# An encoder layer on one core: the first stage's GpSimd tile work on VectorE, two of VectorE's kinds on ScalarE, and level differences one level ahead

## The chip, the core and the metric

The kernel runs on one core of a Trainium2 chip. The core has TensorE (matrix products into PSUM), VectorE and ScalarE (elementwise work), GpSimd (elementwise work, SBUF only) and SyncE (SP), whose queue issues the DMAs here. The metric is the device time of one execution in microseconds.

## The reference

One layer of a bidirectional encoder for 2048 tokens of width 1024. Cut to what matters here:

```
z = rms_norm(x) @ w_in                           # 1024 -> 3424 columns
z_rwkv = z_rwkv + mu * (centred_shift(z_rwkv) - z_rwkv)   # centred_shift: mean of both neighbours
u  = tanh(0.5 * (w0 + tanh(w_lo) @ w_up))        # RWKV decay, as the kernel writes it: exp(-c * (u + 1))
bc = cumsum(log_a) inside a chunk                # GLA, 64 key columns, both directions
scores[i, j] = sum_d q[i, d] * k[j, d] * exp(bc[i, d] - bc[j, d])     # masked to the chunk
o = scores @ v + (q * exp(bc)) @ S
```

`z_rwkv` feeds eight RWKV heads, handled in pairs; the rest of `z` feeds four GLA heads. After the mixers come an output projection, a gated FFN and a gated embedding, each with a norm and a residual.

## The kernel before

Function `phase_a` is the first stage. It goes through the tokens in four quarters `q` of 512. Per quarter it norms and transposes `x` (`make_xn`), then takes 27 projections of 128 columns (`zmat`), each from high and low parts of weights and inputs: three products (`mm3`, lines 73 to 75) per 128-row slice. In the first quarter `weights` loads each slice of `w_in` raw, ScalarE rounds it to the high part (line 217), GpSimd subtracts for the low part (line 218), and both parts are stored to DRAM; the later quarters load them (lines 209 and 210).

`mixed` (lines 294 to 299) makes the shifted mix of a projection: GpSimd adds the two neighbours, VectorE scales the middle, VectorE joins both. It is called 15 times a quarter (60 in all). `rwkv_pair` handles two heads; in each direction ScalarE takes a tanh (line 411), VectorE adds one (line 412, 32 in all) and scans (line 414). `gla_head` makes the scores of one head by levels: the chunk of 128 is halved seven times (`LV`), and at each level the difference of the running sum `b` to the middle of its block is exponentiated (tile `f`) and multiplied with the queries (`qq`) and keys (`kz`); four 128x128 products give a score tile `pl`, and VectorE copies what belongs to the level into `sc` under a mask (line 544). At six levels GpSimd makes two differences of half width (lines 532 and 533), ScalarE the exponential (534), GpSimd the query product (535) and VectorE two key products (536, 537); at the finest level, which comes first, GpSimd's lines are 523, 524 and 526. There are 16 calls of `gla_head`.

Heads (`h`) and pairs (`p`) are interleaved by a list written out by hand (`ORDER`). On top of that the program is laid out with `tile.TileContext(nc, schedule_with_timeline_sim=True)`: a planner puts each engine's instructions in an order from estimated costs, and each engine's queue then keeps that order. Tiles of a pool with one `tag` share its buffers: `f` and `qq` have two, score banks `ps3` three, raw weights `wr` three. The last GLA heads of the last quarter run while the second stage (`phase_b`) starts; its solver uses GpSimd in lines 694 and 695.

Of the kernel before, what the change touches and what calls it, by code (L numbers as in the profile page):

```python
# [7 lines left out]
F32 = mybir.dt.float32  # L8
# [3 lines left out]
AF = mybir.ActivationFunctionType  # L12
ALU = mybir.AluOpType
# [7 lines left out]
TQ = 512  # L21
# [71 lines left out]
def phase_a(ctx, ctr, ctb, tc, k):  # L93

    nc = tc.nc
    V, S, G = nc.vector, nc.scalar, nc.gpsimd
# [15 lines left out]
    ps3 = pool("psd", 3, space=PSUM)  # L112
# [4 lines left out]
    mu1 = c.tile([128, 15], F32, name="mu1")  # L117
# [61 lines left out]
    LV = [64, 32, 16, 8, 4, 2, 1]  # L179

    prev = None
    for li, n in enumerate([128] + LV):
        nb = 128 // n
# [14 lines left out]
    kz = [c.tile([128, TQ], F32, name=f"kz{li}") for li in range(7)]  # L198
# [5 lines left out]
    def weights(ft, first):  # L204

        wh = wp.tile([128, KT, 128], F32R, tag="wh", name="wh")
        wl = wp.tile([128, KT, 128], F32R, tag="wl", name="wl")
        if not first:
            nc.sync.dma_start(wh.bitcast(F32), k.ws[0, ft])
            nc.sync.dma_start(wl.bitcast(F32), k.ws[1, ft])  # L210
            return wh, wl
        n = KT // 2
        for j in range(0, KT, n):
            wr = wp.tile([128, n, 128], F32, tag="wr", bufs=3, name="wr")
            js = slice(j, j + n)
            nc.sync.dma_start(wr, a["w_in"][ft, :, js])
            S.copy(wh[:, js], wr)
            G.tensor_sub(wl[:, js], wr, wh[:, js].bitcast(F32))
        nc.sync.dma_start(k.ws[0, ft], wh.bitcast(F32))
        nc.sync.dma_start(k.ws[1, ft], wl.bitcast(F32))  # L220
        return wh, wl
# [61 lines left out]
    def zmat(ft, x, zp=zp):  # L283

        wh, wl = weights(ft, k.q == 0)
        z = zp.tile([128, XW], F32, tag="z", name="z")
        for (c0, n), (xh, xl) in zip(NB, x):
            pz = ps.tile([128, 512], F32, tag="psz", name="pz")
            for j in range(KT):
                mm3(nc, pz[:, :n], wh[:, j], wl[:, j], xh[:, j], xl[:, j], j == 0, j == KT - 1)  # L290
            S.copy(z[:, c0:c0 + n], pz[:, :n])  # L291
        return z

    def mixed(z, i, out):
        s = pp.tile([128, TQ], F32, tag="s", bufs=2, name="s")
        G.tensor_add(s, z[:, 0:TQ], z[:, 2:TQ + 2])
        V.tensor_scalar(out, z[:, 1:TQ + 1], mu1[:, i:i + 1], None, op0=ALU.mult)
        V.scalar_tensor_tensor(out, s, muh[:, i:i + 1], out, op0=ALU.mult, op1=ALU.add)
        return out

# [45 lines left out]
    def rwkv_pair(q, p, x, lo):  # L346
# [3 lines left out]
        t = lambda tag, bufs=1: pp.tile([128, TQ], F32, tag=tag, bufs=bufs, name=tag)  # L350
# [50 lines left out]
        bv = t("out", 2)  # L401
# [3 lines left out]
        for d in range(2):  # L405
            pu = ps2.tile([128, 512], F32, tag="ps2", name="pu")
            dr = slice(64 * d, 64 * d + 64)
            nc.tensor.matmul(pu, wup[d][:, cs], tw[d], start=True, stop=False)
            nc.tensor.matmul(pu, wupl[dr, cs], tw[d][dr], start=False, stop=True)
            u = t("u", 2)  # L410
            S.activation(u, pu, AF.Tanh, bias=w0h[:, 4 * d + p:4 * d + p + 1], scale=0.5)
            V.tensor_scalar(u, u, 1.0, None, op0=ALU.add)
            rv = (lambda ap: ap) if d == 0 else (lambda ap: ap[:, ::-1])
            V.tensor_tensor_scan(rv(u), m64, rv(u), 0.0, op0=ALU.mult, op1=ALU.add)

            E = pp.tile([128, 8, 65], F32, tag="E", bufs=1, name="E")
            S.activation(E[:, :, 1 - d:65 - d], ch(u), AF.Exp, scale=-0.5 * KAPPA)
            G.memset(E[:, :, 64 * d:64 * d + 1], 1.0)
            S.activation(u, u, AF.Exp, scale=0.5 * KAPPA)
            e1 = 64 if d == 0 else 0  # L420
            S.copy(k.dT[:, p, d, 8 * q:8 * q + 8].unsqueeze(2), E[:, :, e1:e1 + 1])
            st = pp.tile([128, 8, 2, 64], F32, tag="st", bufs=2, name="st")
            V.tensor_mul(st[:, :, 0, :], ch(kk), E[:, :, d:64 + d])
            V.tensor_mul(st[:, :, 1, :], ch(r), E[:, :, 1 - d:65 - d])
            nc.sync.dma_start(k.d["ar"][p, d, :, 8 * q:8 * q + 8], st)
            st = pp.tile([128, 8, 2, 64], F32, tag="st", bufs=2, name="st")
            V.tensor_mul(st[:, :, 0, :], ch(P0), ch(u))
            V.tensor_mul(st[:, :, 1, :], ch(P1), ch(u))
            nc.sync.dma_start(k.d["bk"][p, d, :, 8 * q:8 * q + 8], st)
# [59 lines left out]
    def gla_head(q, h, b, q2, k2, vt):  # L489
        t = lambda tag, bufs=1: gp.tile([128, TQ], F32, tag=tag, bufs=bufs, name=tag)  # L490
        F_, B_ = slice(0, 64), slice(64, 128)
# [16 lines left out]
        tokmajor(kh, kt, ps3, "ps3")  # L508

        sc = t("sc")  # L510
        for li in (6, 0, 1, 2, 3, 4, 5):
            pl = ps3.tile([128, 512], F32, tag="ps3", name="pl")
            n = LV[li]
            tv = lambda ap: ap.rearrange("p (b t) -> p b t", t=2 * n)
            nb = TQ // (2 * n)
            bv, k2v, kv = tv(b), tv(k2), tv(kz[li])
            lhs = kz[li]
            rhs = t("qq", 2)
            f = t("f", 2)
            if li == 6:  # L520

                fv = tv(f)
                G.tensor_sub(fv[F_], bv[F_], bv[F_, :, 0:1].to_broadcast([64, nb, 2]))
                G.tensor_sub(fv[B_], bv[B_, :, 1:2].to_broadcast([64, nb, 2]), bv[B_])
                S.activation(f, f, AF.Exp, scale=0.0625)
                G.tensor_mul(rhs, f, q2)
                V.tensor_copy(kv[F_, :, 0:1], k2v[F_, :, 0:1])
                V.tensor_copy(kv[B_, :, 1:2], k2v[B_, :, 1:2])
            else:
                mid = bv[:, :, n:n + 1].to_broadcast([128, nb, n])  # L530
                fv = tv(f)
                G.tensor_sub(fv[:, :, 0:n], mid, bv[:, :, 0:n])
                G.tensor_sub(fv[:, :, n:2 * n], bv[:, :, n:2 * n], mid)
                S.activation(f, f, AF.Exp, scale=0.0625)  # L534
                G.tensor_mul(rhs, f, q2)  # L535
                V.tensor_mul(kv[F_, :, 0:n], fv[F_, :, 0:n], k2v[F_, :, 0:n])
                V.tensor_mul(kv[B_, :, n:2 * n], fv[B_, :, n:2 * n], k2v[B_, :, n:2 * n])  # L537
            for j in range(4):
                js = slice(128 * j, 128 * j + 128)
                nc.tensor.matmul(pl[:, js], lhs[:, js], rhs[:, js], start=True, stop=True)  # L540
            if li == 6:
                V.tensor_tensor(w4(sc), w4(pl), mk7, op=ALU.mult)
            else:
                V.copy_predicated(w4(sc), msk[:, li, :].unsqueeze(1).to_broadcast([128, 4, 128]), w4(pl))
# [3 lines left out]
        for j in range(4):  # L548
            js = slice(128 * j, 128 * j + 128)
# [4 lines left out]
        for j in range(4):  # L554
            js = slice(128 * j, 128 * j + 128)
# [1012 lines left out]
```

## Time and profile before

| | |
|---|---|
| time, median of 3 runs (lowest, highest) | 3658.14 us (3655.13, 3660.93) |
| profiled execution: its own time, span | 3649.02 us, 3647.3 us |
| TensorE busy, weight loads busy | 3347.8 us (92%), 2856.6 us (78%) |
| VectorE busy | 2624.4 us (72%) |
| ScalarE busy | 1640.8 us (45%) |
| GpSimd busy | 978.7 us (27%) |
| chain that ended last, by engine | TensorE 66%, VectorE 17%, DMA 6%, ScalarE 5%, GpSimd 2% |

Busy time is the time in which an engine has an instruction of its own under way; the time in which its queue waits or issues is not counted. The chain is followed back from the last instruction, at each step to what released it or to the instruction before it on its engine. In the rows PE is TensorE, PEld its weight loads, DVE VectorE, ACT ScalarE, POOL GpSimd, SPq SyncE's queue; `L536` is line 536; `kz<-f,k` says which tile is written from which.

### The profile page before, as it was taken

To read this page: it belongs to the slowest core of one execution; us is meant where nothing else is said; L and a number is where in the kernel's file an instruction comes from. 1 tells how busy PE (TensorE), PEld (TensorE's weight loads), DVE (VectorE), ACT (ScalarE), POOL (GpSimd) and SP (SyncE) were. 2 spreads that over 40 slices of the span, in tenths; PEclk is the share of its full clock that TensorE was granted. 3 is DMA by queue.
4 is the path that set the end of the run, shared out by engine and by line. 5 is a ranking of instruction groups with operands and counts; after the bars stand their busy time and mean duration, and the time that the engine had idled before them with its cause. 6 is when DMAs were issued, how large, how long until landed. Compare 5 with 4: busy or idle time off the path is not lost.

```text
span 3647.3 us, 57330 instructions
## 1 busy us (share of the span) xinstructions
PE 3347.8 (92%) x20880; PEld 2856.6 (78%) x20880; DVE 2624.4 (72%) x4123; ACT 1640.8 (45%) x3451; POOL 978.7 (27%) x1348
## 2 busy tenths in 40 slices
PE   6888988988889899999969989999999999999998
PEld 6777877877878688898858868888788878787776
DVE  6888788788778467776763467777765566769887
ACT  5454445444444555656644453333433333324554
POOL 6854534534335144547401100000000000001112
PEclk9988999999998989999979999999999999999999
DMA  6655465465555445545255655555422234557775
GB/s 219 215 189 184 147 199 187 143 197 170 186 177 175 153 133 156 160 130 155 73 159 169 230 200 185 187 193 191 156 93 81 70 115 150 212 173 272 265 272 185
DMA packets 390439, 629.28 MB, mean 173 GB/s; under 512 B 122790, under 2 KB 223142, under 8 KB 390156
## 3 DMA queue, kind: packets, MB, share of 16 engines
q1 hardware_dynamic: 390156, 625.61, 52.3%
q8 instruction: 165, 2.70, 0.3%
q14 instruction: 118, 0.97, 0.1%
HBM read 403.18 MB, written 211.81 MB: 169 GB/s over the span
## 4 chain that ended last, share of the span: by engine, by line
PE 66%; DVE 17%; DMA 6%; ACT 5%; issue 4%; POOL 2%; SPq 1%; DVEq 0%; ACTq 0%; POOLq 0%
PE pB L73 6%; PE pB L75 6%; PE pB L74 6%; PE pA L74 5%; PE pA L75 4%; PE pA L73 4%; PE pC L74 4%; PE pC L75 4%; PE pC L73 4%; PE pg L662 3%; PE ph L781 3%; PE pf L798 2%; PE pz L75 2%; PE pz L73 2%; PE pz L74 2%
## 5 line engine op out<-in xcount | busy, mean ns | idle before, releaser
L1045 ACT CAST sh<-raws 128x512 fp32r<-128x512 f32 (+1 forms) x456 | 277.6, 610 | 667.0 <-PE pB L74 356.2
L73 PE MATMUL pz<-xh,wh 128*128 128x256 f32 (+1 forms) x1728 | 511.8, 297 | 26.7 <-ACT z L291 18.4
L75 PE MATMUL pz<-xh,wl 128*128 128x256 f32 (+1 forms) x1728 | 504.6, 295 | 6.0 <-DMA wl<-d_ws 4.1
L74 PE MATMUL pz<-xl,wh 128*128 128x256 f32 (+1 forms) x1728 | 504.5, 293 | 0.0
L1210 POOL TENSOR_TENSOR st<-st 128x1 f32<-128x1 f32 x64 | 18.0, 281 | 1631.2 <-ACT jk L1209 1630.7
L1046 DVE TENSOR_TENSOR sl<-raws,sh 128x512 fp32r<-128x512 f32 (+1 forms) x456 | 305.6, 671 | 112.9 <-ACT sh L1045 109.4
L73 PEld LDWEIGHTS pz<-xh,wh 128*128 128x128 f32 x1728 | 339.6, 197 | 40.3 <-ACT z L291 29.1
L75 PEld LDWEIGHTS pz<-xh,wl 128*128 128x128 f32 x1728 | 337.9, 197 | 15.1 <-DMA wl<-d_ws 6.8
L74 PEld LDWEIGHTS pz<-xl,wh 128*128 128x128 f32 x1728 | 340.1, 197 | 6.9 <-issue 5.8
L781 PE MATMUL ph<-x,wpi 128*128 128x128 f32 x1024 | 170.7, 295 | 8.9 <-ACT wpi L777 7.4
L73 PE MATMUL pA<-B11h,sh 128*128 128x512 f32 x360 | 147.7, 411 | 23.0 <-ACT B11h L1045 19.1
L540 PE MATMUL pl<-qq,kz 128*128 128x128 f32 x896 | 133.8, 296 | 32.4 <-DVE kz L537 30.9
L798 PE MATMUL pf<-sv,Ht 128*128 128x64 f32 x1024 | 152.3, 277 | 10.7 <-ACT sv L803 6.9
L540 PEld LDWEIGHTS pl<-qq,kz 128*128 128x128 f32 x896 | 121.2, 208 | 44.0 <-issue 30.2
L781 PEld LDWEIGHTS ph<-x,wpi 128*128 128x128 f32 x1024 | 139.8, 200 | 18.2 <-ACT wpi L777 12.9
L798 PEld LDWEIGHTS pf<-sv,Ht 128*128 128x128 f32 x1024 | 136.0, 196 | 22.5 <-ACT sv L803 10.4
L535 POOL TENSOR_TENSOR qq<-f,q 128x512 f32<-128x512 f32 x96 | 140.7, 1472 | 43.5 <-ACT f L534 24.2
L74 PE MATMUL pA<-B11l,sh 128*128 128x512 f32 x360 | 148.1, 411 | 3.3 <-DVE B11l L1046 3.3
L662 PE MATMUL pg<-ar,bk 64*128 64x128 f32 x1024 | 143.4, 297 | 6.0 <-DVE x L665 4.6
L75 PE MATMUL pA<-B11h,sl 128*128 128x512 f32 x360 | 146.7, 407 | 0.9 <-DVE sl L1046 0.9
L73 PE MATMUL pB<-T3h,sh 128*128 128x512 f32 x360 | 143.4, 398 | 0.0
L75 PE MATMUL pB<-T3h,sl 128*128 128x512 f32 x360 | 143.0, 397 | 0.0
(636 smaller groups left out, 9348.5 us busy)
## 6 DMA issues: line engine op xcount, KB each, us to landing
wh<-d_ws SPq DMA_DIRECT2D x81, 512.0 KB, 4.1
wl<-d_ws SPq DMA_DIRECT2D x81, 512.0 KB, 4.8
d_mt<-rawt SPq DMA_DIRECT2D x92, 256.0 KB, 2.5
raws<-in_ffn_gate SPq DMA_DIRECT2D x44, 512.0 KB, 4.4
raws<-in_ffn_up SPq DMA_DIRECT2D x44, 512.0 KB, 4.0
rawm<-d_mt SPq DMA_DIRECT2D x44, 512.0 KB, 8.6
d_hid<-c SPq DMA_DIRECT2D x88, 256.0 KB, 2.5
d_ar<-st SPq DMA_DIRECT2D x32, 512.0 KB, 2.9
```

The costliest lines, as they stand in the source:

```text
L73: nc.tensor.matmul(out, ah, bh, start=start, stop=False, **kw)
L74: nc.tensor.matmul(out, ah, bl, start=False, stop=False, **kw)
L75: nc.tensor.matmul(out, al, bh, start=False, stop=stop, **kw)
L535: G.tensor_mul(rhs, f, q2)
L540: nc.tensor.matmul(pl[:, js], lhs[:, js], rhs[:, js], start=True, stop=True)
L662: nc.tensor.matmul(pg[h][:, j], bk[HR[h], j], ar[HR[h], j], start=True, stop=True)
L781: nc.tensor.matmul(ph[:, h, j], w[:, h, j], x[:, j0 + j, 4 * h:4 * h + 2, :], start=True, stop=True)
L798: nc.tensor.matmul(pf[:, h, j0 + j], H[:, h, j], SV[p, d, c][:, h, j0 + j], start=True, stop=True)
L1045: nc.scalar.copy(hi, src)
L1046: nc.vector.tensor_sub(lo, src, hi.bitcast(F32))
L1210: G.tensor_add(st[:, 2:3], st[:, 0:1], st[:, 1:2])
```

## The change

All of it is in `phase_a`. Five edits:

- The low part of the weights is subtracted by VectorE in place of GpSimd.
- In `mixed`, VectorE adds the neighbours in place of GpSimd, and ScalarE scales the middle in place of VectorE.
- The add of one in `rwkv_pair` is done by ScalarE in place of VectorE.
- In the level loop of `gla_head` the differences and the query product are done by VectorE in place of GpSimd.
- The differences and the exponential of a level are made by a new function `diff`, which is called one level ahead: before the products of a level, the next level's `f` is begun. The score bank `pl` is asked for after the products.

```diff
--- before.py
+++ after.py
@@ -215,7 +215,7 @@
             js = slice(j, j + n)
             nc.sync.dma_start(wr, a["w_in"][ft, :, js])
             S.copy(wh[:, js], wr)
-            G.tensor_sub(wl[:, js], wr, wh[:, js].bitcast(F32))
+            V.tensor_sub(wl[:, js], wr, wh[:, js].bitcast(F32))
         nc.sync.dma_start(k.ws[0, ft], wh.bitcast(F32))
         nc.sync.dma_start(k.ws[1, ft], wl.bitcast(F32))
         return wh, wl
@@ -293,8 +293,8 @@
 
     def mixed(z, i, out):
         s = pp.tile([128, TQ], F32, tag="s", bufs=2, name="s")
-        G.tensor_add(s, z[:, 0:TQ], z[:, 2:TQ + 2])
-        V.tensor_scalar(out, z[:, 1:TQ + 1], mu1[:, i:i + 1], None, op0=ALU.mult)
+        S.activation(out, z[:, 1:TQ + 1], AF.Copy, scale=mu1[:, i:i + 1])
+        V.tensor_add(s, z[:, 0:TQ], z[:, 2:TQ + 2])
         V.scalar_tensor_tensor(out, s, muh[:, i:i + 1], out, op0=ALU.mult, op1=ALU.add)
         return out
 
@@ -409,7 +409,7 @@
             nc.tensor.matmul(pu, wupl[dr, cs], tw[d][dr], start=False, stop=True)
             u = t("u", 2)
             S.activation(u, pu, AF.Tanh, bias=w0h[:, 4 * d + p:4 * d + p + 1], scale=0.5)
-            V.tensor_scalar(u, u, 1.0, None, op0=ALU.add)
+            S.activation(u, u, AF.Identity, bias=k.one)
             rv = (lambda ap: ap) if d == 0 else (lambda ap: ap[:, ::-1])
             V.tensor_tensor_scan(rv(u), m64, rv(u), 0.0, op0=ALU.mult, op1=ALU.add)
 
@@ -508,33 +508,44 @@
         tokmajor(kh, kt, ps3, "ps3")
 
         sc = t("sc")
-        for li in (6, 0, 1, 2, 3, 4, 5):
-            pl = ps3.tile([128, 512], F32, tag="ps3", name="pl")
+        tv = lambda ap, n: ap.rearrange("p (b t) -> p b t", t=2 * n)
+
+        def diff(li):
+
             n = LV[li]
-            tv = lambda ap: ap.rearrange("p (b t) -> p b t", t=2 * n)
             nb = TQ // (2 * n)
-            bv, k2v, kv = tv(b), tv(k2), tv(kz[li])
+            f = t("f", 2)
+            fv, bv = tv(f, n), tv(b, n)
+            if li == 6:
+
+                V.tensor_sub(fv[F_], bv[F_], bv[F_, :, 0:1].to_broadcast([64, nb, 2]))
+                V.tensor_sub(fv[B_], bv[B_, :, 1:2].to_broadcast([64, nb, 2]), bv[B_])
+            else:
+                mid = bv[:, :, n:n + 1].to_broadcast([128, nb, n])
+                V.tensor_sub(fv[:, :, 0:n], mid, bv[:, :, 0:n])
+                V.tensor_sub(fv[:, :, n:2 * n], bv[:, :, n:2 * n], mid)
+            S.activation(f, f, AF.Exp, scale=0.0625)
+            return f
+
+        levels = (6, 0, 1, 2, 3, 4, 5)
+        nxt = diff(levels[0])
+        for i, li in enumerate(levels):
+            n = LV[li]
+            k2v, kv = tv(k2, n), tv(kz[li], n)
             lhs = kz[li]
             rhs = t("qq", 2)
-            f = t("f", 2)
+            f = nxt
+            if i < 6:
+                nxt = diff(levels[i + 1])
+            fv = tv(f, n)
+            V.tensor_mul(rhs, f, q2)
             if li == 6:
-
-                fv = tv(f)
-                G.tensor_sub(fv[F_], bv[F_], bv[F_, :, 0:1].to_broadcast([64, nb, 2]))
-                G.tensor_sub(fv[B_], bv[B_, :, 1:2].to_broadcast([64, nb, 2]), bv[B_])
-                S.activation(f, f, AF.Exp, scale=0.0625)
-                G.tensor_mul(rhs, f, q2)
                 V.tensor_copy(kv[F_, :, 0:1], k2v[F_, :, 0:1])
                 V.tensor_copy(kv[B_, :, 1:2], k2v[B_, :, 1:2])
             else:
-                mid = bv[:, :, n:n + 1].to_broadcast([128, nb, n])
-                fv = tv(f)
-                G.tensor_sub(fv[:, :, 0:n], mid, bv[:, :, 0:n])
-                G.tensor_sub(fv[:, :, n:2 * n], bv[:, :, n:2 * n], mid)
-                S.activation(f, f, AF.Exp, scale=0.0625)
-                G.tensor_mul(rhs, f, q2)
                 V.tensor_mul(kv[F_, :, 0:n], fv[F_, :, 0:n], k2v[F_, :, 0:n])
                 V.tensor_mul(kv[B_, :, n:2 * n], fv[B_, :, n:2 * n], k2v[B_, :, n:2 * n])
+            pl = ps3.tile([128, 512], F32, tag="ps3", name="pl")
             for j in range(4):
                 js = slice(128 * j, 128 * j + 128)
                 nc.tensor.matmul(pl[:, js], lhs[:, js], rhs[:, js], start=True, stop=True)
```

## Rows read from the trace of the kernel before

**Rows 1.** Windows: stretch, busy us of PE, PEld, DVE, ACT, POOL; clock, DMA, GB/s
```profile
0.00:345.00 345.00, 273.18 (x1864) 247.47 (x1865) 275.17 (x359) 170.42 (x333) 221.49 (x221) 0.92 0.60 199
345.00:617.00 272.00, 242.72 (x1735) 221.35 (x1734) 217.22 (x299) 127.32 (x244) 118.22 (x115) 0.94 0.55 176
...
sum 1190.00, PE 1026.88 PEld 928.01 DVE 946.40 ACT 561.97 POOL 574.96; mean PE 256.72 PEld 232.00 DVE 236.60 ACT 140.49 POOL 143.74
```

**Rows 2.** Chain of waits in the stage: by line, then first and last piece
```profile
by line: issue 7.7%; PE pz L75 6.3%; PE pz L73 6.2%; PE pz L74 6.1%; DVE kz L537 3.5%; PE pl L540 3.1%; DVE kz L536 3.1%; DVE sc L544 2.7%; DMA wl<-d_ws 2.3%; DMA d_bk<-st 2.3%; DVE bx L461 1.9%; DVE bx L460 1.6%; DVE u L414 1.6%; PE po L55
3437 pieces in order of time: start us, us, what
0.73 0.07 issue
...
1189.57 0.48 PE po L557 x2
```

**Rows 3.** Groups of GpSimd in the stage: busy us, mean ns, idle before
```profile
L535 POOL TENSOR_TENSOR qq<-f,q 128x512 f32<-128x512 f32 x96 | 140.7, 1472 | 43.5 <-ACT f L534 24.2 <-PE pl L540 19.1 <-ACT u L411 0.2
L532 POOL TENSOR_TENSOR f<-bx 128x256 f32<-128x256 f32 x96 | 88.7, 924 | 123.2 <-PE pt L305 62.2 <-DVE kz L537 59.1
L218 POOL TENSOR_TENSOR wl<-wr,wh 128x512 fp32r<-128x512 f32 x54 | 81.7, 1527 | 53.5 <-ACT wh L217 51.2 <-issue 2.1
L533 POOL TENSOR_TENSOR f<-bx 128x256 f32<-128x256 f32 x96 | 78.8, 821 | 0.0
L296 POOL TENSOR_TENSOR s<-z 128x512 f32<-128x512 f32 x60 | 72.6, 1209 | 143.8 <-ACT z L291 112.0 <-PE pb L400 27.1 <-DVE kr L298 4.0
L523 POOL TENSOR_TENSOR f<-bx 64x512 f32<-64x512 f32 x16 | 26.2, 1639 | 92.8 <-DVE bx L460 86.8 <-DVE kz L537 5.9
L526 POOL TENSOR_TENSOR qq<-f,q 128x512 f32<-128x512 f32 x16 | 25.7, 1607 | 19.5 <-ACT f L525 10.8 <-DMA q<-qk 7.1 <-PE pz L75 1.5
L524 POOL TENSOR_TENSOR f<-bx 64x512 f32<-64x512 f32 x16 | 25.2, 1572 | 1.1
```

**Rows 4.** VectorE: groups (mean), then lines (min/median/max ns, first and last start)
```profile
L536 DVE TENSOR_TENSOR kz<-f,k 64x256 f32<-64x256 f32 x96 | 68.0, 708 | 17.7 <-ACT f L534 17.3
L497 DVE TENSOR_TENSOR qh<-qh,q 128x512 f32<-128x512 f32 x16 | 15.8, 990 | 5.6 <-ACT qh L496 5.4
L440 DVE SCALAR_TENSOR_TENSOR qk<-cs,cv 128x512 f32<-128x512 f32 x32 | 22.3, 696 | 14.4 <-ACT cs L439 13.9
L271 DVE TENSOR_TENSOR xl<-pt,xh 128x512 fp32r<-128x512 f32 x24 | 16.0, 682 | 0.7 <-ACT xh L270 0.6
...
L536 DVE TENSOR_TENSOR kz<-f,k x96: 391/546/1506, 93.7 to 1177.4; 64x256 f32<-64x256 f32 x96
L440 DVE SCALAR_TENSOR_TENSOR qk<-cs,cv x32: 675/692/907, 67.1 to 1133.9; 128x512 f32<-128x512 f32 x32
L412 DVE TENSOR_SCALAR u<-u x32: 405/426/1519, 151.6 to 1088.9; 128x512 f32<-128x512 f32 x32
L297 DVE TENSOR_SCALAR r<-z,mu x16: 476/502/1505, 97.0 to 1056.5; 128x512 f32<-128x512 f32 x16
L497 DVE TENSOR_TENSOR qh<-qh,q x16: 679/935/1679, 82.4 to 1158.3; 128x512 f32<-128x512 f32 x16
```

**Rows 5.** Line 435 on ScalarE, min/median/max ns
```profile
L435 ACT ACTIVATE cv<-z,pv x32: 706/722/728, 63.5 to 1123.7; 128x512 f32<-128x512 f32 x32
```

**Rows 6.** Waits in the stage: us in total, times, longest (SP's: 0 to 345)
```profile
ACT f L534 <- POOL f L533: 132.8, 58, 6.1
PE pl L540 <- DVE kz L537: 30.9, 19, 4.5
PE pt L305 <- DVE v L298: 18.6, 6, 5.8
DVE kz L536 <- ACT f L534: 17.3, 15, 1.8
SPq L216 <- POOL wl L218: 25.0, 18, 5.2
```

## The prediction

> **What bounds the kernel now.** The page's busy line comes first: TensorE is busy 92% of the span, VectorE 72%, GpSimd 27%. That is an average, so the stage that the change touches is cut out. The last head of the first stage ends shortly after 1190 us, and 1190 us is the stage in all that follows. By windows [rows 1] its TensorE is busy 1027 us (weight loads 928), VectorE 946, ScalarE 562, GpSimd 575. The first window (0 to 345, where the weights are split) is the poorest: TensorE 273 of 345, GpSimd 221. The second is like the two that follow it: TensorE 243 of 272, VectorE 217. No engine is full; two are nearly so, and they wait for each other.
>
> Then the chain of waits in the stage [rows 2]. Its 3437 pieces, added up by engine, are VectorE 477 us, TensorE 376, DMA 95, ScalarE 94, "issue" 91, GpSimd 50. The reader is to see that the three TensorE lines of the projection have 6% each and that directly behind them stand VectorE's two key products of the level loop (L537, L536) and the copy under the mask (L544). VectorE has 1000 us of instructions in the stage when each of its 1311 is counted whole (946 where overlaps count once), so 477/1000 = 0.48 of its work lies on the path; ScalarE's share is 94/562 = 0.17.
>
> Third, GpSimd's groups [rows 3]. The eight kinds that leave are 81.7 + 72.6 + 26.2 + 25.2 + 25.7 + 88.7 + 78.8 + 140.7 = 540 of its 575 us; 35 us stay (roots, memsets, masks, the start of the solver). Last, what single VectorE instructions take [rows 4]. One and the same product L536 takes 391 ns at its shortest and 1506 at its longest, mean 708; the add L412 405 to 1519; L440, which mostly runs when GpSimd rests, 675, median 692. Laid beside GpSimd's spans, the long ones are those that overlap a GpSimd instruction. Two kinds of count give the stretch in all: mean less shortest, over 36 groups with more than half a microsecond (first L536, 68.0 - 96 x 0.391 = 30.5; last L440, 22.3 - 32 x 0.675 = 0.7), is 217 us; with the median of the instructions that meet no GpSimd work in place of the shortest it is 198.
>
> **The change part by part**, against the profiled execution (3649.0 us, span 3647.3; the median of the runs shown is 3658.1, 9.1 more).
>
> *VectorE, what leaves.* The stretch: 198 to 217 us; GpSimd keeps 35 of 575 us, so some 12 may stay, which makes the lower end 188. I take 200. The scaling in `mixed` (60 x 0.476 = 28.6) and the add of one (32 x 0.405 = 13.0) leave with their unstretched length, 42 us; their stretch is in the 200 already [rows 4].
>
> *VectorE, what arrives*, at unstretched lengths, since the partner of the stretching goes. Weight splitting 54 x 0.682, by the like subtraction L271, is 36.8. The neighbour sum in `mixed` 60 x 0.68 (L497 at its shortest, as are the next two) is 40.8; the query products 112 x 0.68 = 76.2; the two subtractions of the finest level 32 x 0.68 = 21.8. The subtractions of the other six levels have 256 columns: 192 x 0.41, just above L536's shortest, = 78.7. Together 254. Below, all at the shortest, it is 250; above, if the new ones were stretched as L536 (0.708) and L497 (15.8/16, 0.99) are now, 391.
>
> Net on VectorE: 254 - 42 - 200 = +12 us, of which 0.48 on the path: **+6**. The ends are 250 - 42 - 217 = -9 (-4 on the path) and 391 - 42 - 188 = +161 (+77); I stay near the low one, since with GpSimd silent the unstretched rows are the nearest.
>
> *GpSimd.* Of its 50 us on the path the moved lines have 45 (f L532 and L533 19, weights 12, products 7, `mixed` 4, finest level 3). It goes: **-45**. What took 0.92 + 0.82 + 1.47 us of GpSimd for a level [rows 3] is 0.41 + 0.41 + 0.68 of VectorE, already counted above. Between zero, if VectorE is just as late there, and -50.
>
> *ScalarE* gets 92 instructions. The nearest row is L435, a scaled copy of the same size with a column operand, 0.722 [rows 5]: 66 us, times 0.17 = **+11**; from 0 (VectorE's own sum runs beside the scaled copy) to all 66. Behind them in its queue stand the projection's evacuations, for which TensorE's next projection waits, so zero is too kind.
>
> What the row shows here is that the column form costs ScalarE 722 ns while VectorE did the two kinds in 476 and 405. The Trainium skill, "ScalarE: Activation LUTs", Rules for kernel authors, says that adds and multiplies belong on VectorE and not on ScalarE. By that rule these two edits lose 66 - 42 = 24 us of engine time, at one common share of 0.48 some 12 us on the path, and the whole sum would be -12. By the rows the engine with the smaller share on the path takes them (-20 + 11), and I go by the rows.
>
> *One level ahead.* ScalarE's exponential of the level loop (0.63 us) had to end before the query product could start; GpSimd's lateness alone cost ScalarE 132.8 us of waiting there, VectorE 17.3 behind the exponential and TensorE 30.9 behind the key products [rows 6]. Now the next level's differences stand ahead of this level's products, so the exponential runs beside 0.68 + 2 x 0.41 + 0.73 us of VectorE work. The 5 us of L534 on the path go: **-5**, from 0 to -17.
>
> *Waits that are added.* The weight subtraction stands on VectorE behind ScalarE's cast. What queues behind it is every head's and pair's work, and SP's loads and stores of weights wait for it as they did for GpSimd (25.0 us before the loads) [rows 6]. GpSimd waited 51.2 us for that cast [rows 3], VectorE in its own like case only 0.7 for 24 [rows 4]; I take under 2 us and keep 51 x 0.48 = 25 as the other end. With two buffers for the level's factor, a next difference must wait for the products of the level before; they are earlier in VectorE's own order, so this costs nothing. The score bank is asked for later, which holds it for less time.
>
> *Order.* The order on every engine is planned anew from estimated costs when the program is made. No row tells the new one; this widens the range alone.
>
> Sum: +6 - 45 + 11 - 5 = **-33 us**: 3616 in the profiled execution, 3625 on the scale of the median. What is late next is VectorE itself, busy about as long as before in a shorter stage, and then TensorE, 163 us idle in it.
>
> **The rivals.**
>
> *VectorE stays the bound.* Its idle 244 us of the stage [rows 1] are ended by TensorE and ScalarE, few of them by GpSimd itself. If that idle share stays and only the work counts, the stage grows with it: 1190 x 12/946 = +15, 3664, on the median's scale 3673. It decides as soon as the stretch is under 254 - 42 = 212 us, and my two counts lie on either side. For it: 946 is close to TensorE's weight loads, and the work of GpSimd was free parallel time. Against it: 45 us of GpSimd on the path and the 17 behind the exponential. The Trainium skill, "Perfetto Trace Analysis", Identifying the Most-Contended Engine, has the same as a rule: the engine with the highest occupancy binds, and TensorE is judged by its weight loads. By that rule the trace names VectorE (946 against 928), and the kernel gets slower. Chance 0.23.
>
> *TensorE is let go.* It waits 122 us for VectorE in the stage, 30.9 of them for the key products and 18.6 for `mixed` values before a transpose [rows 6]. If the first go wholly and the other 91 by half, that is -76: 3573, or 3582. For it: these waits are longest where the stretched instructions are. Against it: VectorE has no less to do. Chance 0.15.
>
> *Nothing to be measured.* The freed path is taken up at once by TensorE, busy 86% [rows 1], and the 45 us of GpSimd by VectorE in its place: 0 to -7, about 3655 on the median's scale. For it: VectorE's sum is level. Chance 0.12.
>
> **How the numbers follow.** Forecast 0.50 (its own range 3590 to 3650), rivals 0.23, 0.15, 0.12. A difference under 0.2% (7.3 us) can't be told from none. Faster: 0.50 + 0.15 = 0.65; the same 0.12; slower 0.23. The range takes in the rival with TensorE let go and 22 us below it, and on the other side the rival with VectorE as the bound: 3560 to 3680. Left out are the far ends of the costs, such as new instructions stretched as the old.
>
> **What would show it.** Right: GpSimd falls from 575 to about 35 us in the stage; L536 and the other all-SBUF groups have means near their shortest; VectorE's busy time stays within 30 us of 946; the wait of the key products on the exponential is gone; the stage ends near 1157. Wrong: stretched VectorE instructions without GpSimd; a VectorE sum of 1000 or more; new TensorE waits for the low weight parts or for ScalarE's evacuations; a stage that ends where it did, with TensorE's idle time unchanged. The rest of the span, 2457 us, should be the same.

## The result, and the profile after

The changed kernel takes 3533.5 us (median of 4 runs, 3530.5 to 3551.8), the one before 3659.5 (a fourth run added to the three above): a ratio of 0.967, 95% interval 0.964 to 0.969, so 126 us faster. Forecast were 3625 and a range from 3560. The direction was right, the size was not: nearly four times the 33 us of the sum.

All of it lies in the stage. In the two profiled executions 2450 us before and 2453 after lie between the last update of the state `SF` (line 558, now 569) and the end; that update is 120 us earlier. Two windows serve for reading what follows: up to 2 us before that update (1195 and 1075 us), and up to the fourth quarter's first cast of `tw` on ScalarE (line 322 in both; 889 and 784 us), before the second stage mixes in. In the runs further down the second window ends at the same cast; "up to the fourth quarter" means it. Columns are as in [rows 1]: stretch, busy us of TensorE, weight loads, VectorE, ScalarE, GpSimd; granted clock, DMA share, GB/s. First the kernel before, then the changed one, whose first two windows answer to the two of [rows 1].

```profile
0.00:889.00 889.00, 756.83 (x5335) 687.41 (x5335) 709.61 (x957) 423.59 (x819) 457.94 (x449) 0.94 0.56 183
0.00:1195.00 1195.00, 1031.88 (x7228) 931.78 (x7228) 949.60 (x1319) 562.71 (x1081) 579.10 (x587) 0.94 0.56 183
```

```profile
0.00:784.00 784.00, 722.12 (x5324) 660.52 (x5325) 689.79 (x1240) 473.78 (x892) 39.63 (x97) 0.97 0.63 207
0.00:1075.00 1075.00, 999.39 (x7282) 907.86 (x7282) 931.67 (x1679) 632.50 (x1188) 53.56 (x142) 0.97 0.62 206
```

```profile
0.00:345.00 345.00, 305.90 (x2266) 282.50 (x2267) 301.66 (x552) 217.59 (x418) 28.61 (x69) 0.97 0.70 234
345.00:617.00 272.00, 264.08 (x1980) 241.60 (x1980) 242.50 (x432) 161.26 (x297) 6.06 (x16) 0.98 0.59 192
```

The reader is to subtract VectorE's busy time from the length. Up to the fourth quarter it was 710 of 889, so 179 us idle; now 690 of 784, 94 idle. Of 105 us gained, 20 are work and 85 idle time. Over the whole stage it is 950 of 1195 (245 idle) against 932 of 1075 (143 idle): 18 and 102. TensorE's granted clock in the stage, a mean over its two levels, rose from 0.94 to 0.97. In the chain of the changed kernel (0 to 1072 us) TensorE's projection lines have 10% each, where [rows 2] has 6%:

```profile
by line: PE pz L73 10.3%; PE pz L75 10.3%; PE pz L74 10.1%; PE pl L551 5.4%; issue 5.2%; DVE qq L541 2.0%; DVE sc L555 2.0%; DMA d_ar<-st 1.9%; PE po L568 1.7%; DMA wh<-d_ws 1.5%; DMA wl<-d_ws 1.4%; PE po L567 1.4%; PE pt L305 1.4%; DVE kz 
4158 pieces in order of time: start us, us, what
```

Summed by engine over these 4158 pieces, TensorE has 514 us (before 376), VectorE 316 (477), GpSimd 1 (50).

Single instructions came out as priced. The groups of VectorE with mean and, last, two lines with shortest, median and longest, against [rows 4]; L541 is the query product, L525 and L526 the differences, L546 the former L536:

```profile
L541 DVE TENSOR_TENSOR qq<-f,q 128x512 f32<-128x512 f32 x112 | 76.6, 684 | 5.6 <-ACT f L527 5.3
L526 DVE TENSOR_TENSOR f<-bx 128x256 f32<-128x256 f32 x96 | 40.4, 421 | 0.0
L525 DVE TENSOR_TENSOR f<-bx 128x256 f32<-128x256 f32 x96 | 40.3, 420 | 1.5 <-PE pt L305 0.8
L297 DVE TENSOR_TENSOR s<-z 128x512 f32<-128x512 f32 x60 | 41.0, 683 | 0.8 <-ACT z L291 0.5
L218 DVE TENSOR_TENSOR wl<-wr,wh 128x512 fp32r<-128x512 f32 x54 | 36.4, 689 | 12.5 <-ACT wh L217 12.1
L546 DVE TENSOR_TENSOR kz<-f,k 64x256 f32<-64x256 f32 x96 | 39.9, 416 | 2.6 <-ACT f L527 2.2
L497 DVE TENSOR_TENSOR qh<-qh,q 128x512 f32<-128x512 f32 x16 | 11.0, 684 | 0.2
...
L546 DVE TENSOR_TENSOR kz<-f,k x96: 406/412/558, 87.0 to 1064.1; 64x256 f32<-64x256 f32 x96
L497 DVE TENSOR_TENSOR qh<-qh,q x16: 659/685/694, 76.9 to 1047.9; 128x512 f32<-128x512 f32 x16
```

The 54, 60, 112, 192 and 32 new instructions take 257 us (254 forecast); the 32 of the finest level, not shown, have 22 of them. L546 now runs from 406 to 558 ns, where L536 ran from 391 to 1506. Mean less shortest, over all groups of the stage, fell from 217 to 24 us. The two kinds on ScalarE take the 0.72 us that [rows 5] said:

```profile
L412 ACT ACTIVATE u<-u,one 128x512 f32<-128x512 f32 x32 | 23.1, 721 | 0.3
L296 ACT ACTIVATE r<-z,mu 128x512 f32<-128x512 f32 x16 | 11.6, 723 | 10.6 <-DVE st L424 10.6
```

GpSimd is all but silent up to the fourth quarter (40 us; 54 in the stage, about 35 forecast), against [rows 3]. Its two largest groups:

```profile
L236 POOL TENSOR_TENSOR st<-st,mhalf 128x1 f32<-128x1 f32 (+1 forms) x17 | 15.2, 894 | 102.5 <-DVE st L235 102.4
L200 POOL MEMSET kz<- 128x512 f32 x7 | 4.0, 601 | 0.1
```

The waits that answer to [rows 6]:

```profile
ACT f L527 <- DVE f L526: 91.5, 53, 3.9
DVE wl L218 <- ACT wh L217: 12.1, 6, 4.9
DVE qq L541 <- ACT f L527: 5.3, 6, 1.8
PE pl L551 <- DVE kz L547: 4.6, 4, 2.8
PE pt L305 <- DVE v L298: 0.9, 1, 0.9
```

The first is long, but ScalarE has slack (474 busy of 784 us). The second is the added wait for the cast, priced under 2 us: VectorE waited 12.1. TensorE's wait for the key products fell from 30.9 to 4.6 us, the one for `mixed` values before a transpose from 18.6 to 0.9; all its waits for VectorE in the stage from 122 to 52. VectorE's own waits, put together by the engine named in them, fell from 126 to 73 us for ScalarE, from 68 to 34 for TensorE and from 13 to 5 for GpSimd. The largest of them, before and after:

```profile
DVE SF L558 <- PE po L557: 26.6, 20, 4.0
```

```profile
DVE SF L569 <- PE po L568: 14.9, 15, 3.3
```

### The profile page after: what moved, and what is told of

Same layout as the page of the kernel before. It is cut to its first block, busy times and chain, and to the rows that moved or that the text cites. A ratio compares the mean times of both kernels' runs of the same rounds, so it can differ in the third digit from the quotient of the medians.

```text
span 3529.9 us, 57042 instructions
## 1 busy us (share of the span) xinstructions
PE 3322.2 (94%) x20880; PEld 2839.5 (80%) x20880; DVE 2607.5 (74%) x4481; ACT 1705.3 (48%) x3547; POOL 450.5 (13%) x898
## 4 chain that ended last, share of the span: by engine, by line
PE 73%; DVE 12%; DMA 7%; ACT 4%; issue 3%; SPq 1%; POOL 0%; DVEq 0%; ACTq 0%; POOLq 0%
PE pB L73 7%; PE pB L75 6%; PE pB L74 6%; PE pA L74 5%; PE pA L75 5%; PE pA L73 5%; PE pC L74 4%; PE pC L75 4%; PE pC L73 4%; PE pz L73 3%; PE pz L75 3%; PE pz L74 3%; PE pg L673 3%; PE ph L792 3%; PE pf L809 2%
## 5 line engine op out<-in xcount | busy, mean ns | idle before, releaser
L73 PE MATMUL pz<-xh,wh 128*128 128x256 f32 (+1 forms) x1728 | 501.0, 291 | 13.3 <-DMA wh<-d_ws 7.1
L75 PE MATMUL pz<-xh,wl 128*128 128x258 f32 (+1 forms) x1728 | 495.9, 290 | 5.6 <-DVE wl L218 3.1
L74 PE MATMUL pz<-xl,wh 128*128 128x256 f32 (+1 forms) x1728 | 496.5, 288 | 0.2 <-DVE xl L271 0.2
L73 PEld LDWEIGHTS pz<-xh,wh 128*128 128x128 f32 x1728 | 330.9, 192 | 22.6 <-issue 13.7
L75 PEld LDWEIGHTS pz<-xh,wl 128*128 128x128 f32 x1728 | 328.2, 191 | 15.9 <-issue 6.8
L74 PEld LDWEIGHTS pz<-xl,wh 128*128 128x128 f32 x1728 | 331.5, 192 | 6.3 <-issue 5.3
L74 PE MATMUL pB<-T3l,sh 128*128 128x512 f32 x360 | 142.5, 396 | 0.0
L1056 ACT CAST sh<-s 128x512 fp32r<-128x512 f32 (+1 forms) x76 | 46.3, 609 | 186.6 <-PE pA L74 164.0
L673 PEld LDWEIGHTS pg<-ar,bk 64*128 64x128 f32 x1024 | 119.4, 196 | 19.5 <-DVE x L676 4.2
```

Source lines behind the costliest of these rows:

```text
L73: nc.tensor.matmul(out, ah, bh, start=start, stop=False, **kw)
L74: nc.tensor.matmul(out, ah, bl, start=False, stop=False, **kw)
L75: nc.tensor.matmul(out, al, bh, start=False, stop=stop, **kw)
L673: nc.tensor.matmul(pg[h][:, j], bk[HR[h], j], ar[HR[h], j], start=True, stop=True)
L1056: nc.scalar.copy(hi, src)
```

## Experiments

The time of VectorE up to the fourth quarter is split into busy and idle throughout; the windows have the columns above. "Changed" is the changed kernel. Its own repeat on a later chip (after_again) was 0.968 of before, 0.963 to 0.973.

**Idle work for GpSimd**, with the old amount of reading, for nobody (beside the low weight parts too, in the same way):

```diff
         V.tensor_add(s, z[:, 0:TQ], z[:, 2:TQ + 2])
+        for j in (0, 256):
+            G.tensor_add(junk, z[:, j:j + 256], z[:, j + 2:j + 258])
...
+            for j in (0, 256):
+                G.tensor_sub(junk, b[:, 0:256], b[:, 256:512])
             S.activation(f, f, AF.Exp, scale=0.0625)
...
             V.tensor_mul(rhs, f, q2)
+            for j in (0, 256):
+                G.tensor_mul(junk, b[:, j:j + 256], q2[:, j:j + 256])
```

> The changed kernel, and beside it GpSimd again does its old amount of SBUF work (as twice as many instructions of half the size), into a scratch tile that nobody reads; it waits only for tiles that stay alive anyway. So VectorE can be stretched as before, but nobody waits for GpSimd. Stretch theory (VectorE's instructions grow while GpSimd reads SBUF, and the grown ones are those that TensorE waits for): most of the 126 us come back, 3600 to 3660 us, and the product on the level's keys has a mean near 0.7 us again. Lateness theory (the level loop waited for GpSimd's results): nobody waits for GpSimd here, so 3530 to 3565.

3765.3 us, 1.031 of before (1.029 to 1.033):

```profile
0.00:985.00 985.00, 787.14 (x5388) 711.23 (x5388) 880.71 (x1241) 475.79 (x893) 562.16 (x635) 0.89 0.50 166
```

VectorE is busy 881 us, 191 more than in the changed kernel, and idle 104, 10 more. So stretch is real and costs its full length, not 0.48 of it: the fourth quarter begins 201 us later. (TensorE's granted clock fell to 0.89 as well; but VectorE waited only 10 us longer, so the delay is VectorE's.) The whole is 105 above the upper end of the forecast. There is more GpSimd work than before (562 us in the window against 458) and more VectorE work to stretch; which of the two makes it was not taken apart.

**The level loop on GpSimd again**, one level ahead:

```diff
-                V.tensor_sub(fv[:, :, 0:n], mid, bv[:, :, 0:n])
-                V.tensor_sub(fv[:, :, n:2 * n], bv[:, :, n:2 * n], mid)
+                G.tensor_sub(fv[:, :, 0:n], mid, bv[:, :, 0:n])
+                G.tensor_sub(fv[:, :, n:2 * n], bv[:, :, n:2 * n], mid)
...
-            V.tensor_mul(rhs, f, q2)
+            G.tensor_mul(rhs, f, q2)
```

> The changed kernel with the level loop's differences and query products on GpSimd again, still one level ahead; the weights, the mix and the two ScalarE kinds stay as changed. GpSimd then has 386 of its 540 us back. Stretch theory: 386/540 of 126 = 90 us come back, about 3620. Lateness theory: the differences are a level ahead, so only the query product's 1.5 us is late: 3550 to 3590.

3619.5 us, 0.991 (0.988 to 0.993), 86 above the changed kernel. The first number was right and its reason was not:

```profile
0.00:859.00 859.00, 744.24 (x5357) 673.83 (x5357) 692.42 (x992) 465.43 (x886) 327.73 (x349) 0.97 0.57 190
```

VectorE is as busy as in the changed kernel (692 against 690): what is stretched (123 us, mean less shortest) makes up for what left. It is idle 167 us against 94. The 73 us are lateness. Its granted clock is 0.97, as in the changed kernel, so the higher clock by itself is not what makes the changed kernel faster.

**Without the level ahead**: the level's differences and exponential stand in the level itself, as before, and the score bank is asked for ahead of them again.

```diff
-        nxt = diff(levels[0])
...
-                nxt = diff(levels[i + 1])
...
+                V.tensor_sub(fv[:, :, 0:n], mid, bv[:, :, 0:n])
+                V.tensor_sub(fv[:, :, n:2 * n], bv[:, :, n:2 * n], mid)
+                S.activation(f, f, AF.Exp, scale=0.0625)
+                V.tensor_mul(rhs, f, q2)
```

> The changed kernel without the level ahead: each level's differences stand in the level itself, all on VectorE. Stretch theory: GpSimd is silent, so 3533 to 3550. Lateness theory: VectorE or TensorE now waits for the exponential at 112 levels, about 0.8 us each, some 90 us if nothing fills them: 3570 to 3620.

3576.7 us, 0.979 (0.976 to 0.983), 43 slower than changed:

```profile
0.00:795.00 795.00, 722.67 (x5370) 663.64 (x5371) 691.15 (x1241) 475.10 (x894) 41.22 (x97) 0.98 0.62 206
```

Only 11 us of it stand before the fourth quarter, 10 of them idle time, and 13 before the last state update. Some 25 us came after it, in code that is the same (2477 us against 2453, in the profiled executions). That is read below.

**The low weight parts on GpSimd again**:

```diff
-            V.tensor_sub(wl[:, js], wr, wh[:, js].bitcast(F32))
+            G.tensor_sub(wl[:, js], wr, wh[:, js].bitcast(F32))
```

> The changed kernel with the low weight parts on GpSimd again (first quarter alone, 54 subtractions). Stretch theory: 82/540 of 126 = 19 us slower, about 3552, all in the first quarter. Lateness theory: a wait of the low parts only, 3530 to 3540, or a few us faster because VectorE is rid of 37 us.

3558.2 us, 0.974 (0.971 to 0.976), 25 slower:

```profile
0.00:818.00 818.00, 731.52 (x5329) 668.39 (x5330) 700.39 (x1186) 468.74 (x887) 120.94 (x151) 0.96 0.60 199
```

VectorE is 11 us busier though 37 us of work left it, and idle 23 us more. Moving the work off VectorE was a loss on both counts.

**The level loop alone**: before, with the changed kernel's `diff` and loop, all on VectorE and one level ahead. The edit as it differs from the changed kernel, whose other parts are taken back:

```diff
-            V.tensor_sub(wl[:, js], wr, wh[:, js].bitcast(F32))
+            G.tensor_sub(wl[:, js], wr, wh[:, js].bitcast(F32))
...
-        S.activation(out, z[:, 1:TQ + 1], AF.Copy, scale=mu1[:, i:i + 1])
-        V.tensor_add(s, z[:, 0:TQ], z[:, 2:TQ + 2])
+        G.tensor_add(s, z[:, 0:TQ], z[:, 2:TQ + 2])
+        V.tensor_scalar(out, z[:, 1:TQ + 1], mu1[:, i:i + 1], None, op0=ALU.mult)
...
-            S.activation(u, u, AF.Identity, bias=k.one)
+            V.tensor_scalar(u, u, 1.0, None, op0=ALU.add)
```

> The kernel before with one part of the change: the level loop's differences and query products on VectorE, one level ahead. GpSimd keeps the weights and the mix, VectorE its two kinds. Busy-plus-idle theory (the stage lasts as long as VectorE is busy, stretch counted in full, plus some 140 us of idle time where the heads don't wait for GpSimd, some 225 to 245 where they do): busy 952 + 177 that arrive - 386/540 of 200 = 986, idle 150, stage 1136, so 61 faster, about 3595. Share theory (0.48 of VectorE's work on the path, as in the prediction): +16 - 29 - 5 = -18, about 3637.

3613.3 us, 0.985 (0.981 to 0.989), 46 faster than before, between the two forecasts:

```profile
0.00:842.00 842.00, 748.57 (x5389) 682.00 (x5390) 726.12 (x1209) 431.56 (x826) 179.41 (x198) 0.95 0.59 195
```

VectorE's idle time fell from 179 to 116 with GpSimd still busy 179 us. The last state update stands at 1136 us, 61 earlier than before and just where busy plus idle had it (977 busy and 159 idle; 986 and 150 forecast, so that two misses of 9 cancel); the time after it was 25 us longer than before, in the same code.

**The two ScalarE kinds back on VectorE** (the scaling in `mixed` and the add of one):

```diff
-        S.activation(out, z[:, 1:TQ + 1], AF.Copy, scale=mu1[:, i:i + 1])
+        V.tensor_scalar(out, z[:, 1:TQ + 1], mu1[:, i:i + 1], None, op0=ALU.mult)
...
-            S.activation(u, u, AF.Identity, bias=k.one)
+            V.tensor_scalar(u, u, 1.0, None, op0=ALU.add)
```

> The changed kernel with the scaling in the mix and the add of one back on VectorE. Busy-plus-idle theory: VectorE has 42 us more, unstretched, and the stage that much longer: about 3575. Share theory: at the share of VectorE on the changed kernel's path, 0.31, less ScalarE's share: +13 - 7, about 3540.

3540.2 us, 0.966 (0.962 to 0.969): no difference from changed that these runs tell.

```profile
0.00:797.00 797.00, 721.51 (x5343) 663.64 (x5344) 714.74 (x1308) 427.57 (x821) 39.22 (x97) 0.96 0.61 204
```

VectorE is 25 us busier up to the fourth quarter and 12 less idle: the quarter begins 13 us later. Work put on VectorE is no longer paid in full.

**The two kinds alone** (before, with these two on ScalarE):

```diff
-        V.tensor_scalar(out, z[:, 1:TQ + 1], mu1[:, i:i + 1], None, op0=ALU.mult)
+        S.activation(out, z[:, 1:TQ + 1], AF.Copy, scale=mu1[:, i:i + 1])
...
-            V.tensor_scalar(u, u, 1.0, None, op0=ALU.add)
+            S.activation(u, u, AF.Identity, bias=k.one)
```

> The kernel before with one part of the change: the scaling in the mix and the add of one on ScalarE; everything of GpSimd stays. Busy-plus-idle theory: VectorE loses 42 us and the 28 by which these two kinds are stretched, so about 70 faster, 3585; if other instructions are stretched in their place, 42: 3612. Share theory: -34 + 11 = -23, about 3632.

3645.1 us, 0.996 (0.993 to 0.999): 14 faster, less than any of the three numbers.

```profile
0.00:862.00 862.00, 747.77 (x5351) 679.74 (x5352) 669.57 (x892) 466.33 (x888) 456.48 (x449) 0.95 0.58 189
```

VectorE's busy time fell by 40 up to the fourth quarter and its idle time rose by 13. The last state update is 36 us earlier than before, near the 42 of busy plus idle; the time after it is 32 us longer (2482 against 2450), and so little is left of it in the whole.

**The level ahead alone** (before, with the changed kernel's `diff` and loop, in which the work stays on GpSimd):

```diff
+            if i < 6:
+                nxt = diff(levels[i + 1])
+            fv = tv(f, n)
+            G.tensor_mul(rhs, f, q2)
```

> The kernel before with one part of the change: the level loop one level ahead, everything still on GpSimd. If what GpSimd cost was only that its differences and the exponential came late, the idle time of VectorE falls from 245 to about 150 us and the kernel is some 90 us faster, 3565. If what counts is that the query product and the key products go back and forth between GpSimd and VectorE, it gains under 20 us, 3635 to 3655, as the changed kernel with the level loop on GpSimd, whose idle time of 225 us was hardly less, lets expect.

3661.7 us, 0.999 (0.997 to 1.002): nothing. VectorE is idle 180 us, as before:

```profile
0.00:891.00 891.00, 755.90 (x5337) 685.89 (x5337) 711.42 (x957) 424.11 (x820) 458.30 (x449) 0.94 0.56 183
```

**Half the loop each.** Changed, with the differences on GpSimd, and changed, with the query product there:

```diff
-                V.tensor_sub(fv[:, :, 0:n], mid, bv[:, :, 0:n])
-                V.tensor_sub(fv[:, :, n:2 * n], bv[:, :, n:2 * n], mid)
+                G.tensor_sub(fv[:, :, 0:n], mid, bv[:, :, 0:n])
+                G.tensor_sub(fv[:, :, n:2 * n], bv[:, :, n:2 * n], mid)
```

```diff
-            V.tensor_mul(rhs, f, q2)
+            G.tensor_mul(rhs, f, q2)
```

> The changed kernel with only the level differences on GpSimd (one level ahead); the query product stays on VectorE. Up to the fourth quarter VectorE is idle 94 us in the changed kernel and 167 with the whole level loop on GpSimd. If the query product's way over GpSimd and back makes that idle time, it stays near 105 here; VectorE's work is 100 us less and some 80 us of stretch more, so 3520 to 3545. If late differences make it, it is near 165 and the kernel near 3590.

> The changed kernel with only the query product on GpSimd; the differences stay on VectorE, one level ahead. If the product's way over GpSimd and back makes the idle time of VectorE, it is near 165 us up to the fourth quarter and the kernel near 3590. If the differences make it, it stays near 105; VectorE's work is 77 us less and some 61 us of stretch more, so 3520 to 3545.

3563.9 us, 0.974 (0.969 to 0.978), and 3566.6, 0.974 (0.970 to 0.979). First the differences on GpSimd, then the product:

```profile
0.00:807.00 807.00, 734.37 (x5381) 666.44 (x5382) 682.80 (x1082) 468.45 (x896) 200.81 (x266) 0.97 0.61 203
```

```profile
0.00:820.00 820.00, 733.86 (x5351) 666.79 (x5352) 709.71 (x1162) 468.50 (x893) 171.32 (x182) 0.97 0.60 199
```

Idle times are 124 and 110. Neither half makes the 73 us by itself: 30 and 16, and the rest appears only when both stand in one loop on GpSimd's queue. Both expectations gave an idle time near 165 or near 105 and a kernel of 3590 or under 3545; neither run is at either.

**Handover without work**, and **work without a handover**, in the level loop:

```diff
+            G.tensor_copy(f[:, 0:1], f[:, 0:1])
             V.tensor_mul(rhs, f, q2)
```

```diff
                 V.tensor_sub(fv[:, :, n:2 * n], bv[:, :, n:2 * n], mid)
+            for j in (0, 256):
+                G.tensor_sub(junk, b[:, 0:256], b[:, 256:512])
...
             V.tensor_mul(rhs, f, q2)
+            for j in (0, 256):
+                G.tensor_mul(junk, b[:, j:j + 256], q2[:, j:j + 256])
```

> The changed kernel, but between a level's exponential and its products GpSimd copies one column of the factor onto itself: a handover to GpSimd and back 112 times, with next to no GpSimd work. If the handovers themselves made VectorE idle, most of the 73 us of idle time (up to the fourth quarter) and of the 86 us come back, 3590 to 3610. If the length of GpSimd's stretched instructions made it, little does: 3535 to 3560.

> The changed kernel with idle GpSimd work in the level loop alone, as much as the level loop's own (differences and query product, into a scratch tile), and nobody waits for it. VectorE keeps all its work. Up to the fourth quarter: VectorE's stretch is some 125 us, as with the level loop on GpSimd, or more, its idle time near 100 and not 167, and the quarter begins 110 to 150 us later than in the changed kernel; the whole 3640 to 3690. If stretch were a small matter, 3540 to 3570.

Handover: 3543.8 us, 0.971 (0.965 to 0.976). The copies and the window:

```profile
L541 POOL COPY f<-f 128x1 f32<-128x1 f32 x84 | 55.5, 662 | 529.6 <-ACT f L527 520.0 <-ACT xh L270 9.4
```

```profile
0.00:795.00 795.00, 729.30 (x5389) 669.83 (x5389) 690.52 (x1241) 473.25 (x893) 99.43 (x181) 0.97 0.63 206
```

Idle 104: the 84 trips to GpSimd and back in the window cost 10 us, though a copy of one column lasts 662 ns here. So it is not the handover as such; what is left is how long GpSimd's work in the loop takes. With the loop on GpSimd its instructions are, per level, two of 0.9 and one of 1.5 us in one queue:

```profile
L541 POOL TENSOR_TENSOR qq<-f,q 128x512 f32<-128x512 f32 x84 | 124.3, 1484 | 71.8 <-DMA q<-qk 33.3 <-ACT f L527 24.2 <-PE pl L551 12.8
L525 POOL TENSOR_TENSOR f<-bx 128x256 f32<-128x256 f32 x72 | 66.2, 920 | 136.6 <-PE pt L305 75.7 <-DVE kz L547 58.9
L526 POOL TENSOR_TENSOR f<-bx 128x256 f32<-128x256 f32 x72 | 64.4, 894 | 0.0
```

Work without a handover: 3739.5 us, 1.021 (1.016 to 1.026); the window, then GpSimd's idle work:

```profile
0.00:930.00 930.00, 773.58 (x5325) 703.10 (x5326) 837.89 (x1240) 474.53 (x892) 371.84 (x433) 0.91 0.53 175
```

```profile
L529 POOL TENSOR_TENSOR junk<-bx 128x256 bf16<-128x256 f32 x168 | 171.2, 1019 | 174.0 <-DVE bx L462 161.7
L546 POOL TENSOR_TENSOR junk<-bx,q 128x256 bf16<-128x256 f32 x168 | 164.5, 979 | 12.6
```

and of VectorE the copy under the mask (L560) and the key product (L551):

```profile
L560 DVE COPY_PREDICATED sc<-msk,pl 128x512 f32<-128x512 uint8 x72 | 52.7, 731 | 0.6 <-PE pl L556 0.2
L551 DVE TENSOR_TENSOR kz<-f,k 64x256 f32<-64x256 f32 x72 | 42.9, 596 | 0.8 <-ACT f L530 0.5
```

With 336 us of GpSimd work in the window, VectorE is 148 us busier than in the changed kernel and idle 92: no lateness, all stretch. The quarter begins 146 us later, as forecast; the whole is 50 us above the upper end of its forecast. The key product has a mean of 596 ns, against 416 when GpSimd is silent. The copy under the mask, whose data come from PSUM, takes 731 ns here, 731 in the kernel before and 734 in the changed one:

```profile
L544 DVE COPY_PREDICATED sc<-msk,pl 128x512 f32<-128x512 uint8 x96 | 70.2, 731 | 13.5 <-PE pl L540 11.8 <-DVE sc L544 0.5
```

```profile
L555 DVE COPY_PREDICATED sc<-msk,pl 128x512 f32<-128x512 uint8 x96 | 70.4, 734 | 0.6
```

**Lighter**: more of VectorE's work on ScalarE.

```diff
-        V.tensor_scalar(sq, pss, 1e-24, None, op0=ALU.max)
-        S.activation(sq, sq, AF.Ln)
+        S.activation(sq, pss, AF.Ln, bias=tiny)
...
-        V.tensor_scalar(ta, ta, kah[:, p:p + 1], ka1[:, p:p + 1], op0=ALU.mult, op1=ALU.add)
+        S.activation(ta, ta, AF.Identity, scale=kah[:, p:p + 1], bias=ka1[:, p:p + 1])
...
-                V.tensor_copy(kv[F_, :, 0:1], k2v[F_, :, 0:1])
+                S.copy(kv[F_, :, 0:1], k2v[F_, :, 0:1])
```

> The changed kernel with more of VectorE's work on ScalarE: the scaling of the gate in the pairs (16), the two key copies of the finest level (32), and the floor under the root's logarithm, which becomes a bias of the logarithm (16 VectorE instructions less, for any sum of squares that isn't tiny the same value). VectorE loses 16 x 0.545 + 32 x 0.29 + 16 x 0.69 = 29 us. Where VectorE's work counts in full it is 29 faster, about 3505; if the changed kernel's stage is by now as much TensorE's, as the 42 us of the two kinds put back on VectorE (7 us slower) say, 5 faster, about 3528.

3547.1 us, 0.970 (0.964 to 0.975), and beside it, on the same chip, the changed kernel:

> The changed kernel again, unaltered, beside the others on the same chip: 3533 by its first measurement, so that a few us between it and the lighter one can be read.

3542.4 us, 0.968 (0.963 to 0.973). No gain. The lighter kernel, then the changed one on that chip:

```profile
0.00:787.00 787.00, 720.88 (x5337) 662.09 (x5338) 671.89 (x1193) 490.26 (x926) 42.58 (x97) 0.96 0.64 207
```

```profile
0.00:788.00 788.00, 723.31 (x5322) 663.52 (x5323) 689.84 (x1240) 473.07 (x891) 39.57 (x97) 0.97 0.62 206
```

VectorE's busy time fell by 18, its idle time rose by 17. VectorE's waits for ScalarE in this window rose from 54 to 79 us: what left VectorE came back as lateness of the engine that took it. No run was measurably faster than the changed kernel.

## Why the prediction was wrong

*What held.* The price of every instruction that moved (254 forecast, 257 measured; 0.72 on ScalarE). The stretch: 200 us taken, 193 gone by the same count (217 less 24; the 217 are all groups, the 36 largest alone have 215). VectorE's whole sum (each instruction counted in full, up to the last state update), forecast 12 us up, rose from 1005 to 1025. The rest of the span: 2457 us was to stay the same, and from the last state update on it was 2450 before and 2453 after.

*What failed* is the step that turned work into time. The prediction took the share of an engine's time on the chain of waits as the price of its work: 0.48 for VectorE, and 45 us for GpSimd because 45 us of its instructions stood there. In its place the runs showed that VectorE's busy time and its idle time have each a price of their own, and that the idle time was the larger part: 102 of the 120 us.

The term for GpSimd was mis-sized: -45, with -50 as its far end, and -5 for the level ahead, against 102 us of VectorE's idle time that went (85 up to the fourth quarter). That most of this is GpSimd's lateness in the level loop was shown (73 of the 85 us came back with the loop alone on GpSimd): up to the fourth quarter VectorE idles with the loop on GpSimd 179, 180, 192 and 167 us in four kernels (before, ahead_alone, two_scalar_alone, heads_gpsimd), with the whole loop on VectorE 82 to 118 in ten, among them idle_gpsimd with 104, whose GpSimd is busier than before's. The waits name GpSimd for little of it: of VectorE's waits in the stage 8 us for GpSimd went, and 87 for ScalarE and TensorE. A late product would be followed by such waits; before, VectorE's largest was for TensorE in the state update (26.6 us, now 14.9), with no GpSimd in the row. Which wait goes back to which GpSimd instruction was not traced.

The term for VectorE, +6, came out small by luck: it is the difference of large terms that nearly cancel, and VectorE's busy time, overlaps counted once, fell by 18 us. Its factor was wrong. Where the two idle-work runs put stretch alone on VectorE, it came out up to the fourth quarter at full length, 191 and 148 us of busy time for 201 and 146 us of delay. Had the removed stretch not been there to pay for the 257 us that arrive, the change would, by these sums, have been slower (257 - 42 = 215 us more work in the stage, 102 of idle time less). In the other direction the factor fails too: in the changed kernel 42 us of work put back cost 13 us up to the fourth quarter (25 of busy time) and nothing measurable in the whole, and work taken off gains nothing. TensorE is busy 722 of 784 us there, and the lighter kernel waits longer for ScalarE; how much of it is which, no run tells.

*ScalarE*, +11, can't be seen as a term of its own: its busy time in the stage rose from 562 to 632 us, and its time on the chain fell from 94 to 67. The two kinds together, forecast at -20 + 11, gave 36 us in the stage when moved alone.

*The level ahead*, -5: on GpSimd it gains nothing; on VectorE 11 us up to the fourth quarter, with the later request for the score bank in it.

*The rivals.* "VectorE stays the bound" at an unchanged idle share fell: its sum rose by 20 us and the stage is 120 shorter. The Trainium skill, "Perfetto Trace Analysis", Identifying the Most-Contended Engine, was named beside it. Its rule, the highest occupancy, fits the stage before: VectorE is busiest there (946 us against 928 of weight loads), and 54 us taken off it alone made the stage 36 shorter. The rival failed by the idle share that it kept: 20% of the stage before, 13% after. "TensorE is let go", at 0.15, was the nearest: it foresaw -76 by TensorE's waits for VectorE, and these fell by 70. It left out that VectorE's own waits fall too.

On the stretch the Trainium skill, "SBUF — State Buffer", Who interferes with whom, says that a VectorE instruction with two SBUF inputs contends with a GpSimd instruction that reads SBUF, for ports which the two engines share and which only one of them can hold at a time. The runs agree: 416 ns for the key product with GpSimd silent, 596 with idle work, and 734 and 731 ns for the copy from PSUM. That sentence speaks of two inputs; the add of one, with a single one, was stretched too, from 405 to as much as 1519 ns [rows 4].

*What stays open.* Why each half of the loop on GpSimd makes 30 and 16 us of idle time and both make 73; a queue that is late for the next level as well would do it, but no run took it apart. And the code after the last state update, the same in all, took from 2434 to 2482 us. What differs there is TensorE's busy time, 2306 to 2347 us, and not VectorE's, 1668 to 1676. With no_ahead it is 2345 us at a mean granted clock of 0.95, in the changed kernel 2321 at 0.96: 24 of the 25 us. Executions of one kernel differ in the same way: the slowest of the kernel before took 3686 us at a mean clock of 0.947, its fastest 3646 at 0.957. Why the clock was lower is open, and whether the order on each engine, which is planned anew for each kernel, has a part in it was not tried. So some 25 of no_ahead's 43 us say little of the level ahead, and the stage is the better measure of every part.

## What to carry to other kernels

Split the time of the engine that does most into busy and idle, and price a change for both: work moved on or off it, with the stretch by other engines, counts in full while it is the bound, and idle time is what late results cost, whichever engine the waits name. An engine's own share on the chain of waits said little here about what its lateness costs. How much idle time would go was not foreseen from rows: the forecast for the level loop alone, which met the stage, took its idle time from the changed kernel. Two tests tell them apart: the work without anybody waiting for it, and the wait without the work.

## What was not expected of the hardware

Work on GpSimd that nobody waits for made the kernel 6% slower than changed (206 us; 336 us of such work up to the fourth quarter delayed that quarter by 146). A GpSimd copy of one column took 662 ns in the mean where VectorE was busy beside it.
